# Attention's transposes, mLSTM products and P·V sums share one rotation of four PSUM banks

## The chip, the core and the metric

The kernel runs on one NeuronCore of a Trainium2 chip. Its engines work in parallel, each through its own queue in order: TensorE (PE) with its weight loads (PEld), VectorE (DVE), ScalarE (ACT), GpSimd (POOL), and SyncE (SP), which here issues all DMA transfers. PE writes its results to PSUM, of which this program uses eight banks of 2 KB per partition; DVE and ACT read them out. The metric is the device time of one execution in microseconds (us), lower is better, given as a median over runs.

## The reference, cut to what matters

One layer: a normed and modulated input projection, then two groups of heads side by side (window attention and a two-directional mLSTM), a joint output projection, and a SwiGLU block. The change lies in the part between the two projections:

```python
def window_attention(q, k, v, kc, vc, sink):
    # 8 query heads on 2 key heads, 8 blocks of 128 queries; keys: three neighbouring blocks and 256 context keys
    s_loc = where(valid, einsum(q_block, k_band) * scale, -inf);  s_ctx = einsum(q_block, k_context) * scale
    m = max(s_loc.max, s_ctx.max, sink)
    p_loc, p_ctx = exp(s_loc - m), exp(s_ctx - m)
    inv = 1 / (p_loc.sum + p_ctx.sum + exp(sink - m))
    o = einsum(p_loc * inv, v_band) + einsum(p_ctx * inv, v_context)

def mlstm_chunkwise(q, k, v, ig, lf, state):      # 4 heads, once forward and once backward
    s = einsum(q, k) * w_intra
    num = einsum(s, v) + w_inter * einsum(C, q);  den = s.sum + w_inter * einsum(n, q)
    h = num / max(abs(den), exp(-m))
```

All inputs are float32, 1024 latent tokens and 256 context tokens, width 1024.

## The kernel before, in words

The program has three stretches. The first (to about 293 us of the span) computes modulation, projections, gates and the mLSTM states. The second (about 293 to 457 us) is the attention with the mLSTM outputs, and the first part of the output projection. The third (457 us to the end) is the rest of the output projection and the SwiGLU block, as a Strassen-like product.

In the second stretch the work is cut into 16 **items** (n, g): block of 128 queries n, key head g. For each item `Soft` makes the scores of four heads (L973, L974 on PE into a two-bank tile `s`; the DVE reduction L975 reads it, adds the mask and takes the extreme), the exponentials (ACT, L984) and the division by the row sum (POOL, L989). Two items later `Values.tr` transposes the four heads of one key tile on PE into a bank `pt` (L1002, five tiles `T0` to `T4` per inner item), and copies it to SBUF as `ts_`, even tiles on ACT (L1007), odd ones on DVE (L1005). After both items of a block, `pv` sums the products of P and V for all key tiles into one bank (L1020), and `pv_out` copies that to `mix` on ACT (L1026).

Into the first eight items the mLSTM of blocks 0 to 7 is woven: `ml_scores` (L862, tile `s`, then DVE L867), `ml_values` once per direction (L876 and L880 into two banks `pt`, read by DVE L885 to L887 and by ACT L892 or DVE L894), `ml_norm` (ACT L901 to L903, POOL L904), and `ml_out`, which transposes four heads into one bank `pt` (L910) for DVE L911.

What is issued for one item stands as letters in the plans `PLAN_ML`, `PLAN` and `PLAN13` (T transposes, A scores, N exponentials and division, V mLSTM values, z mLSTM output, M0 and M1 the two calls of `pv` with key tiles 0 to 2 and 3 to 4, O the copy out). From these a scheduler that models the engines sets the order of instructions on each engine, and where it gives a tile one of its buffers. Within one `pv` call the products keep their order. From `msplit(0, 1)` after the loop the order is the program's own.

PSUM before: tag `s` has two buffers of two banks; tag `pt` three of one bank, for transposes and mLSTM products; tag `po` one bank, for the P·V sum. The third stretch uses the same tags, `bank()` for `pt` and `two_banks()` for `pt` with `po`.

Of the kernel before, what the change touches and what calls it, by code (L numbers as in the profile page):

```python
# [9 lines left out]
F32 = mybir.dt.float32  # L10
# [3 lines left out]
PSUM = bass.MemoryType.PSUM  # L14
ADD, SUB, MUL, MAX, MIN = ALU.add, ALU.subtract, ALU.mult, ALU.max, ALU.min

P = 128
D = 1024
# [26 lines left out]
def body(tc, x, ctx, vecs, bcv, bada, gqm, gqf, wada, ws1, ws2, wt, wout, wfi, wfo,  # L45
# [5 lines left out]
    def open_pool(name, bufs=1, side="left", space=None):  # L51
        kw = dict(name=name, bufs=bufs, reuse_waits="tile")
        if space is not None:
            kw["space"] = space
        else:
            kw["side"] = side
        p = tc.tile_pool(**kw)
        return p, p.__enter__()

    def close(p):  # L60
        p[0].__exit__(None, None, None)
# [65 lines left out]
    def R(k, name, shape, dt=F32):  # L127
        t = rp[1].tile([P, 1152 if k < 4 else 1024], dt, name=name, tag=f"r{k}")
        n = int(np.prod(shape))
        v = t[:, 0:n]  # L130
        if len(shape) == 2:
            v = v.rearrange("p (a b) -> p a b", b=shape[1])
        elif len(shape) == 3:
            v = v.rearrange("p (a b c) -> p a b c", b=shape[1], c=shape[2])
        elif len(shape) == 4:
            v = v.rearrange("p (a b c d) -> p a b c d", b=shape[1], c=shape[2], d=shape[3])
        return v
# [160 lines left out]
    for sec in (1, 0):  # L298
# [52 lines left out]
        for q in range(2):  # L351
            t = (hcol, scol)[sec][:, q]
# [70 lines left out]
    for i in range(NI):  # L423
# [16 lines left out]
        if i in (1, 2):  # L440
            b = i - 1
# [138 lines left out]
    def T(i, name):  # L580
        return q2.tile([P, S], F32, name=name, tag=f"s{i}")
# [159 lines left out]
    for j, name in enumerate(TILES):  # L741
# [10 lines left out]
        elif name == "ak":  # L752
# [5 lines left out]
            for a, b, w, dst in ((kr, ks, S, slice(0, S)), (kc[:, 0:L], kc[:, L:2 * L], L, slice(S, S + L))):  # L758
                t = th[64:P] if w == S else kc[64:P, 2 * L:3 * L]
# [7 lines left out]
        elif name.startswith("aq"):  # L767
            t = T(0, f"aq{i}")
# [6 lines left out]
        else:  # L775
            t = R(14 if i == 3 else 15, "so", (S,))
# [39 lines left out]
    pb = psB[1]  # L816
# [4 lines left out]
    qa = atp[1]  # L821
    qa.tile([P, 4, P], F32, name="ts_", tag="pts", bufs=NTS)
    qa.tile([P, 80], F32, name="padq")
    for x_, n in (("pt", 3), ("po", 1)):
        pb.tile([P, 4, P], F32, name=x_, tag=x_, bufs=n)

    def bank():
        return pb.tile([P, 4, P], F32, name="pt", tag="pt", bufs=3)

    def two_banks():  # L830
        return [t.rearrange("p a b -> p (a b)") for t in (bank(), pb.tile([P, 4, P], F32, name="po", tag="po", bufs=1))]


    wts, qps, hss, qz = {}, {}, {}, {}
# [34 lines left out]
    def ml_values(n, d):  # L869
        wt_, qp_, hs = wts[n], qps[n], hss[n][0]  # L870
        s_, r0 = rows_of(n, d)
        cs = state(d, s_)
        pv = [bank().rearrange("p a b -> p (a b)")[:, 0:258].rearrange("p (j v) -> p j v", j=2) for hb in range(2)]
        for j in range(2):
            for hb in range(2):
                pe.matmul(pv[hb][:, j, :], qp_[:, d, j, hb, :], cs[:, j, :], start=j == 0, stop=False,  # L876
                          skip_group_check=j > 0)
        for hb in range(2):
            for j in range(2):
                pe.matmul(pv[hb][:, j, :], wt_[:, d, 2 * j + hb, :], V[:, n, 2 * j + hb, :], start=False, stop=True,  # L880
                          skip_group_check=j > 0)
        dn = qa.tile([P, 2, 2], F32, name="dn", tag="dn", bufs=4)
        for hb in range(2):
            den = pv[hb][:, :, 128]
            dve.tensor_tensor(dn[:, hb], den, emcol[:, r0 + hb:r0 + 4:2], MAX)  # L885
            dve.scalar_tensor_tensor(dn[:, hb], den, -1.0, dn[:, hb], MUL, MAX)
        dve.reciprocal(dn, dn)  # L887
        for hb in range(2):
            for j in range(2):
                t = hs[:, 2 * j + hb]  # L890
                if d == 0:
                    act.activation(t, pv[hb][:, j, 0:128], AF.Copy, scale=dn[:, hb, j:j + 1])  # L892
                else:
                    dve.scalar_tensor_tensor(t, pv[hb][:, j, 0:128], dn[:, hb, j:j + 1], t, MUL, ADD)  # L894
# [11 lines left out]
    def ml_out(n):  # L906
        hs, so = hss.pop(n)
        pt = bank()
        for h in range(4):
            pe.transpose(pt[:, h, :], hs[:, h, :], ident)  # L910
        dve.tensor_tensor(mix[n][:, 4:8, :], pt, so, MUL)  # L911
# [97 lines left out]
    pos = {}  # L1009

    def pv(a, b, ts, more, pin=True):

        ts = [t for t in ts if t < a.nt][::-1]
        first = a.n not in pos
        if first:
            pos[a.n] = pb.tile([P, 4, P], F32, name="po", tag="po", bufs=1)
        for t in ts:
            vt = a.kb0 + t if t < a.nb else NT + t - a.nb
            for g, x_ in ((1, b), (0, a)):
                r = pe.matmul(pos[a.n][64 * g:64 * g + 64], av[:, vt, g], x_.p.pop(t), start=first and t == ts[0],  # L1020
                              stop=not more and t == ts[-1])
                if pin and (t != ts[0] or not g):
                    tc.keep_in_program_order(r)

    def pv_out(n):
        act.copy(mix[n][:, 0:4, :], pos.pop(n))  # L1026
# [3 lines left out]
    for i in range(2):  # L1030
        a = Soft(i)
# [25 lines left out]
    b = None  # L1057
    for i in range(NIT):
        a = Soft(i + 2) if i + 2 < NIT else None
        b0, b = b, Values(i)  # L1060
# [5 lines left out]
        for k in (PLAN_ML[i % 2] if i < NT else PLAN13 if i == NIT - 3 else PLAN[i % 2]).split():  # L1066
            op, n = k[0], int(k[1:] or 0)
            if op == "w" and i + 1 < NT:
                ml_load(i + 1)
            elif op == "T" and n < b.nt:  # L1070
                b.tr(n)
            elif op == "M" and i % 2:
                pv(b0, b, ((0, 1, 2), (3, 4))[n], not n)
            elif op == "O" and i % 2:
                pv_out(b.n)
            elif op == "A" and a:
                a.scores(n)
            elif op == "N" and a:
                a.norm(n)
            elif op == "V" and i < NT:  # L1080
                ml_values(i, n)
            elif op == "x" and i < NT:
                ml_norm(i)
            elif op == "s" and i + 1 < NT:
                ml_scores(i + 1)
            elif op == "z" and 1 <= i <= NT:
                ml_out(i - 1)
            elif op == "l":
                for j in WLOADS.get(i, ()):
                    wout_load(j)  # L1090
            elif op == "p" and i in WSPLIT:
                wout_split(i)
            elif op == "m":
                msplit(0, 0)
                ops_[0] = pb.tile([P, 1024], F32, name="op", tag="s", bufs=2)
            elif op == "P":
                omm(0, 0, range(n, n + 1))
# [17 lines left out]
    msplit(1, 1)  # L1115
    act.preload_act_table_set("sqrt_and_others")
    pv(b, b2, range(4), False, False)
    omm(0, 1, range(3, 4))
    ops_[1] = pb.tile([P, 1024], F32, name="op", tag="s", bufs=2)
    omm(1, 1, range(4))  # L1120
    pv_out(b.n)
    order.__exit__(None, None, None)
    close(atp)
    close(aqp)
    close(akp)
# [142 lines left out]
    def mm_fi(ps, w, b, first):  # L1268

        for k in range(4):  # L1270
            mm3(ps, (w[:, 0, k], w[:, 1, k]), b[k], first and k == 0, k == 3, more=not first)

    def bop(x):
        return [(bh[x][0][:, k], bh[x][1][:, k]) for k in range(4)]

    xv, zb, tm_ = {}, {}, {}

    def fi1(p):
        if p == 2:
            xv[p] = two_banks()  # L1280
        else:
            t = pb.tile([P, D], F32, name=f"xv{p}", tag="s", bufs=2)
            xv[p] = [t[:, 0:512], t[:, 512:D] if p else pb.tile([P, 512], F32, name="xv0b", tag="po", bufs=1)]
        mm_fi(xv[p][0], wops[p]["11"], bop("11"), True)

    def fi2(p):
# [81 lines left out]
    tsums(2, (0, 1))  # L1368
    tsp("T2", 0, 2, "h")
    fi1(0)  # L1370
    opost1(N1)
    es0 = prp[1].tile([P, 512], F32, name="es0", tag="mh", bufs=2)
# [7 lines left out]
    fi2(0)  # L1380
    xstore(N1)
    fi1(1)
    otr(N1)
    close(pC)
# [134 lines left out]
    def gacc(k):  # L1519

        if k < KT:
            dve.scalar_tensor_tensor(gt["acc"], gt[k], csil[:, k, 0:1], gt["acc"], MUL, ADD)
            return
        gps = two_banks()
        for i in range(2):
            sl = slice(i * 512, (i + 1) * 512)
            ps = gps[i]
            for p_ in range(2):
                pe.matmul(ps, gt["one"], gt["hl"][:, p_, sl], start=not p_, stop=p_ == 1)
            gt["p", i] = ps  # L1530
# [193 lines left out]
    for p in range(4, HT):  # L1724
# [39 lines left out]
        if not end:  # L1764
            fm(p + 1, 1)
        else:
            X4 += two_banks()
            t = pb.tile([P, D], F32, name="fx2", tag="s", bufs=2)
            X4 += [t[:, 0:512], t[:, 512:D]]
            fstep(0)  # L1770
# [95 lines left out]
    for s_ in range(1, 8):  # L1866
        q0 = (s_ - 1) * NJ
        KL = 4 if s_ == 7 else 2
        if s_ == 2:
            t = pb.tile([P, D], F32, name="fy0", tag="s", bufs=2)  # L1870
# [35 lines left out]
    close(h2p)  # L1906
    close(prp)
    close(rp)
    close(psB)
    close(cp)  # L1910

# [79 lines left out]
```

## Time and profile before

| | |
|---|---|
| time, median of 3 runs | 1181.61 us (1180.16 to 1184.69) |
| the profiled execution | 1181.65 us, its span 1179.9 us |
| PE busy over the span | 1161.8 us (98%) |
| first stretch, 0 to 293 us | PE busy 286.01 us |
| second stretch, 293 to 457 us | PE busy 159.00 of 164.00 us, DVE 111.27, ACT 115.51, POOL 81.82 |
| third stretch, 457 to 1180 us | PE busy 716.77 of 723.00 us |

A row of a timeline gives start, length, engine, line, operation, output and inputs, and the count of merged instructions; in brackets stands the idle time before it and who ended it. Matmuls overlap, so the time that one takes from the next is read from start to start, not from its length. A float32 P·V product shows as two matmul records of 128x512.

### The profile page before, as it was taken

How to read it: one execution, taken by the hardware profiler on the slowest of the kernel's cores; microseconds unless marked ns; L12 is line 12 of the kernel's file. 1: busy time of each engine (PE TensorE's matmuls, PEld its weight loads, DVE VectorE, ACT ScalarE, POOL GpSimd, SP SyncE). 2: the span in 40 equal slices, each digit the busy share in tenths (PEclk: the TensorE clock that was granted, in tenths of full speed). 3: DMA queues.
4: the chain of work that ended last, by engine and by line, in shares of the span. 5: the costliest groups of instructions: out<-in, count | busy, mean ns of one | idle time of the engine just before them, and what ended most of it. 6: DMA issues, size and time to landing. Idle time of an engine off the chain costs nothing.

```text
span 1179.9 us, 16215 instructions
## 1 busy us (share of the span) xinstructions
PE 1161.8 (98%) x5881; PEld 947.8 (80%) x5881; DVE 781.5 (66%) x1367; ACT 557.7 (47%) x1035; POOL 153.9 (13%) x204
## 2 busy tenths in 40 slices
PE   8899999999999999999999999999999999999997
PEld 3799888778787777888788888888888888888886
DVE  5863768872877752559777767777777755644566
ACT  6743442221776864887443333333333435434543
POOL 1550001225555650000000000000000000000000
PEclk9999999999999999999999999999999999999999
DMA  9611954647887613220233565655654558666853
GB/s 366 218 54 52 391 191 140 216 122 226 217 259 194 200 56 142 90 90 36 98 134 130 202 238 207 221 197 205 221 172 135 178 192 276 201 214 190 303 185 125
DMA packets 101992, 214.89 MB, mean 182 GB/s; under 512 B 10004, under 2 KB 39316, under 8 KB 100504
## 3 DMA queue, kind: packets, MB, share of 16 engines
q1 hardware_dynamic: 101912, 213.85, 54.5%
q8 instruction: 46, 0.75, 0.3%
q14 instruction: 34, 0.28, 0.1%
HBM read 157.19 MB, written 55.97 MB: 181 GB/s over the span
## 4 chain that ended last, share of the span: by engine, by line
PE 89%; DVE 4%; DMA 4%; ACT 1%; issue 1%; SPq 0%; POOL 0%; DVEq 0%; ACTq 0%
PE xv L79 8%; PE xv L78 8%; PE xv L77 8%; PE pt L79 6%; PE pt L77 6%; PE pt L78 6%; PE po L1020 3%; PE t L597 3%; PE t L596 3%; PE t L599 3%; PE pt L1002 3%; PE op L77 3%; PE op L79 2%; PE op L78 2%; PE fx L77 2%; PE slab L77 2%
## 5 line engine op out<-in xcount | busy, mean ns | idle before, releaser
L66 DVE TENSOR_TENSOR fo<-fr,fo 128x1024 fp32r<-128x1024 f32 x77 | 92.9, 1223 | 70.2 <-ACT fo L65 68.4
L65 ACT CAST fo<-fr 128x1024 fp32r<-128x1024 f32 x77 | 79.7, 1053 | 73.9 <-PE pt L79 36.4
L596 PE MATMUL t<-hh,th 128*128 128x512 f32 x208 | 82.4, 396 | 0.0
L597 PE MATMUL t<-hl,th 128*128 128x512 f32 x208 | 82.1, 395 | 0.0
L1397 ACT CAST wS<-wr 128x512 fp32r<-128x512 f32 x88 | 54.3, 624 | 55.2 <-PE pt L79 36.7
L1399 DVE TENSOR_TENSOR wS<-wr,wS 128x512 fp32r<-128x512 f32 x88 | 60.4, 689 | 19.8 <-ACT wS L1397 19.8
L79 PE MATMUL xv<-tT,wS 128*128 128x512 f32 x168 | 65.6, 391 | 0.0
L77 PE MATMUL xv<-tT,wS 128*128 128x512 f32 x168 | 65.6, 390 | 0.0
L78 PE MATMUL xv<-tT,wS 128*128 128x512 f32 x168 | 65.5, 390 | 0.0
L599 PE MATMUL t<-hh,tl 128*128 128x512 f32 x208 | 65.0, 393 | 0.0
L77 PE MATMUL op<-woh,mh 128*128 128x512 f32 x128 | 51.1, 400 | 0.0
L79 PE MATMUL op<-woh,ml 128*128 128x512 f32 x128 | 50.0, 391 | 0.0
L78 PE MATMUL op<-wol,mh 128*128 128x512 f32 x128 | 49.9, 390 | 0.0
L1145 DVE TENSOR_TENSOR wr<-wr 128x512 f32<-128x512 f32 x66 | 45.5, 689 | 1.4
L596 PEld LDWEIGHTS t<-hh,th 128*128 128x128 f32 x208 | 39.1, 188 | 8.3 <-issue 0.3
L597 PEld LDWEIGHTS t<-hl,th 128*128 128x128 f32 x208 | 39.1, 188 | 8.1 <-issue 1.4
L1431 ACT ACTIVATE es<-es 128x512 f32<-128x512 f32 x22 | 14.0, 634 | 66.5 <-DVE es L1148 66.5
L78 PE MATMUL pt<-fo 128*128 128x512 f32 x110 | 42.8, 389 | 0.0
L77 PE MATMUL pt<-fo 128*128 128x512 f32 x110 | 42.8, 389 | 0.0
L79 PE MATMUL pt<-fo 128*128 128x512 f32 x110 | 42.8, 389 | 0.0
L599 PEld LDWEIGHTS t<-hh,tl 128*128 128x128 f32 x208 | 37.3, 188 | 6.6 <-issue 0.5
L973 PE MATMUL s<-k,qh 128*128 128x256 f32 (+1 forms) x128 | 41.7, 337 | 0.6 <-DVE sm L975 0.5
(786 smaller groups left out, 3340.2 us busy)
## 6 DMA issues: line engine op xcount, KB each, us to landing
wr<-in_wfi SPq DMA_DIRECT2D x44, 512.0 KB, 4.7
wb<-in_wada SPq DMA_DIRECT2D x24, 512.0 KB, 5.6
s_d<-a SPq DMA_DIRECT2D x22, 512.0 KB, 7.0
bt<-in_wfo SPq DMA_DIRECT2D x44, 256.0 KB, 3.6
tb_d<-bt SPq DMA_DIRECT2D x11, 1024.0 KB, 3.9
fr<-s_d SPq DMA_DIRECT2D x44, 256.0 KB, 4.2
fr<-tb_d SPq DMA_DIRECT2D x44, 256.0 KB, 4.0
fr<-a_d SPq DMA_DIRECT2D x33, 256.0 KB, 4.3
```

The costliest lines, as they stand in the source:

```text
L65: act.copy(hi, raw)
L66: dve.tensor_tensor(lo, raw, hi.bitcast(F32), SUB)
L77: pe.matmul(ps, a[0], b[0], start=first, stop=False, **kw)
L78: pe.matmul(ps, a[0], b[1], start=False, stop=False, **kw)
L79: pe.matmul(ps, a[1], b[0], start=False, stop=last, **kw)
L596: pe.matmul(o, wh[:, kt], m[0], start=f, stop=False)
L597: pe.matmul(o, wh[:, kt], m[1], start=False, stop=False)
L599: pe.matmul(o, wl[:, kt], m[0], start=False, stop=l)
L973: pe.matmul(o, qh[:, h, :], k2[g][:, kc], start=True, stop=False)
L1145: dve.tensor_tensor(out, a, b, SUB)
L1397: act.copy(w[:, 0], raw)
L1399: dve.tensor_tensor(w[:, 1], raw, w[:, 0].bitcast(F32), SUB)
```

## The change

`po` goes out of the first pool, and a new pool `psT` with four buffers of tag `pt` stands beside it during attention. The P·V sum of a block is now one more tile of that rotation: `pv` takes it with `bank()` when the first batch is issued, it is kept over the second batch, and it is free again once `pv_out` has copied it. The score tiles `s` keep their two buffers, in a pool of their own. When the hand-ordered end of attention is through, `psT` is closed, and a pool `psT2` with three buffers `pt` and one `po` takes its place for the third stretch, whose code is the same but for the name of the tile. No instruction is added or removed on a compute engine; the scheduler, with other buffers to give, puts the second stretch in another order.

```diff
-    for x_, n in (("pt", 3), ("po", 1)):
-        pb.tile([P, 4, P], F32, name=x_, tag=x_, bufs=n)
+    pb.tile([P, 1024], F32, name="s", tag="s", bufs=2)
+    psT = open_pool("psT", space=PSUM)
+    nbk = [4]
+    psT[1].tile([P, 4, P], F32, name="pt", tag="pt", bufs=4)

     def bank():
-        return pb.tile([P, 4, P], F32, name="pt", tag="pt", bufs=3)
+        return psT[1].tile([P, 4, P], F32, name="pt", tag="pt", bufs=nbk[0])
+
+    def po_bank():
+        return psT[1].tile([P, 4, P], F32, name="po", tag="po", bufs=1)

     def two_banks():
-        return [t.rearrange("p a b -> p (a b)") for t in (bank(), pb.tile([P, 4, P], F32, name="po", tag="po", bufs=1))]
+        return [t.rearrange("p a b -> p (a b)") for t in (bank(), po_bank())]
...
         if first:
-            pos[a.n] = pb.tile([P, 4, P], F32, name="po", tag="po", bufs=1)
+            pos[a.n] = bank()
...
     pv_out(b.n)
     order.__exit__(None, None, None)
+    close(psT)
+    psT = open_pool("psT2", space=PSUM)
+    nbk[0] = 3
+    for x_, n in (("pt", 3), ("po", 1)):
+        psT[1].tile([P, 4, P], F32, name=x_, tag=x_, bufs=n)
```

What this does to the order shows at two places on PE. In the changed kernel the lines of this stretch stand five lower in the file: PE's L867 is the former L862, L881 L876, L885 L880, L915 L910, L978 and L979 L973 and L974, L1007 L1002, L1025 L1020. Texts below name lines by their old numbers.

First, PE around `ml_out` of block 3 (`hs3`). Numbers behind a name tell buffers of one name apart. Before:

```order
L1002 MATMUL pt_3530<-vec_59,pr__3138 128x128 x4
L876 MATMUL pt_3537<-cs2_2357,qz0_2731 128x129 x2
L880 MATMUL pt_3537<-V_88,wl4_3429 128x129 x2
L973 MATMUL s_3653<-k2_1_1331,qh_3475 128x384
L974 MATMUL s_3653<-k2_1_1331,ql_3476 128x384
L973 MATMUL s_3653<-k2_1_1331,qh_3475 128x256
L974 MATMUL s_3653<-k2_1_1331,ql_3476 128x256
L876 MATMUL pt_3538<-cs2_2357,qz0_2731 128x129 x2
L880 MATMUL pt_3538<-V_88,wl4_3429 128x129 x2
L1002 MATMUL pt_3562<-vec_59,pr__3138 128x128 x4
L910 MATMUL pt_3569<-vec_59,hs3_3267 128x128 x4
```

And in the changed kernel:

```order
L881 MATMUL pt_3540<-cs2_2357,qz0_2734 128x129 x2
L885 MATMUL pt_3540<-V_88,wl4_3432 128x129 x2
L867 MATMUL s_3606<-mq0_1340,mk0_1338 128x128 x2
L867 MATMUL s_3606<-mq1_1341,mk1_1339 128x128 x2
L978 MATMUL s_3650<-k2_1_1331,qh_3478 128x384
L979 MATMUL s_3650<-k2_1_1331,ql_3479 128x384
L978 MATMUL s_3650<-k2_1_1331,qh_3478 128x256
L979 MATMUL s_3650<-k2_1_1331,ql_3479 128x256
L881 MATMUL pt_3541<-cs2_2357,qz0_2734 128x129 x2
L885 MATMUL pt_3541<-V_88,wl4_3432 128x129 x2
L1007 MATMUL pt_3565<-vec_59,pr__3141 128x128 x4
L915 MATMUL pt_3572<-vec_59,hs3_3270 128x128 x4
```

In both, the mLSTM values of block 4 (two tiles), a transposed key tile and the output of block 3 follow each other: four tiles `pt`, which before have three buffers and now four. The mLSTM scores (L862, now L867) have moved ahead of the group's scores.

Second, PE at the first P·V sum (block 0). Before:

```order
L880 MATMUL pt_3033<-V_88,wl1_2937 128x129 x2
L1020 MATMUL po_3064<-ts__3030,av_91 64x512
L1020 MATMUL po_3064<-ts__2883,av_91 64x512
L973 MATMUL s_3006<-k2_1_1331,qh_2834 128x384
L974 MATMUL s_3006<-k2_1_1331,ql_2835 128x384
L973 MATMUL s_3006<-k2_1_1331,qh_2834 128x256
L974 MATMUL s_3006<-k2_1_1331,ql_2835 128x256
L1002 MATMUL pt_3057<-vec_59,pr__2794 128x128 x4
L1020 MATMUL po_3064<-ts__3023,av_91 64x512
L1020 MATMUL po_3064<-ts__2876,av_91 64x512
L1020 MATMUL po_3064<-ts__2992,av_91 64x512
L1020 MATMUL po_3064<-ts__2845,av_91 64x512
```

And in the changed kernel:

```order
L1007 MATMUL pt_3060<-vec_59,pr__2797 128x128 x4
L885 MATMUL pt_3035<-V_88,wl1_2940 128x129 x2
L1025 MATMUL pt_3067<-ts__3033,av_91 64x512
L1025 MATMUL pt_3067<-ts__2886,av_91 64x512
L1025 MATMUL pt_3067<-ts__3026,av_91 64x512
L1025 MATMUL pt_3067<-ts__2879,av_91 64x512
L1025 MATMUL pt_3067<-ts__2995,av_91 64x512
L1025 MATMUL pt_3067<-ts__2848,av_91 64x512
L885 MATMUL pt_3036<-V_88,wl1_2940 128x129 x2
```

The first batch of this sum stood in two pieces, with scores and a transpose between them, and now stands in one. Over the stretch PE's order has 18 groups of P·V rows before and 15 now, with the same number of products.

More of the change, by code (lines that the diff above doesn't have):

```diff
@@ L1282, in fi1 @@
             t = pb.tile([P, D], F32, name=f"xv{p}", tag="s", bufs=2)
-            xv[p] = [t[:, 0:512], t[:, 512:D] if p else pb.tile([P, 512], F32, name="xv0b", tag="po", bufs=1)]
+            xv[p] = [t[:, 0:512], t[:, 512:D] if p else po_bank().rearrange("p a b -> p (a b)")]
         mm_fi(xv[p][0], wops[p]["11"], bop("11"), True)
@@ L1908, in body @@
     close(rp)
+    close(psT)
     close(psB)
```

## The prediction

> **What bounds the kernel now.** I read the page's busy shares first, then its chain of waits.
>
> ```profile
> PE 1161.8 (98%) x5881; PEld 947.8 (80%) x5881; DVE 781.5 (66%) x1367; ACT 557.7 (47%) x1035; POOL 153.9 (13%) x204
> PE 89%; DVE 4%; DMA 4%; ACT 1%; issue 1%; SPq 0%; POOL 0%; DVEq 0%; ACTq 0%
> ```
>
> PE is busy for 98% of the span and holds 89% of the chain that ended last. An edit that removes no PE work can win only what PE loses in the stretch that it touches. The windows of the three stretches, and the slice of the second in which DVE is fullest (columns: length, then busy time of PE, PEld, DVE, ACT, POOL, granted clock, DMA share, GB/s):
>
> ```profile
> 0.00:293.00 293.00, 286.01 (x1591) 232.76 (x1592) 193.03 (x357) 116.74 (x200) 71.14 (x100) 0.99 0.59 198
> 293.00:457.00 164.00, 159.00 (x1110) 123.82 (x1108) 111.27 (x347) 115.51 (x306) 81.82 (x104) 1.00 0.63 181
> 457.00:1180.00 723.00, 716.77 (x3186) 591.26 (x3182) 477.23 (x663) 325.46 (x529) 0.96 (x1) 1.00 0.51 176
> 320.00:340.00 20.00, 19.38 (x155) 17.43 (x152) 18.15 (x63) 15.93 (x48) 9.80 (x11) 1.00 0.81 226
> ```
>
> In the 164 us of attention PE idles 5.0 us (164.00 - 159.00). The list of PE's waits in that stretch names nearly all of it (waiter, awaited, total us, times, longest):
>
> ```profile
> PE po L1020 <- DVE ts__4746 L1005: 0.8, 1, 0.8
> PE pt L910 <- ACT ts__3567 L1007: 0.8, 1, 0.8
> PE pt L910 <- ACT ts__3893 L1007: 0.8, 1, 0.8
> PE pt L910 <- ACT ts__3233 L1007: 0.5, 1, 0.5
> PE s L973 <- DVE sm L975: 0.5, 1, 0.5
> PE s L974 <- DMA ql<-aq_dl: 0.5, 1, 0.5
> PE pt L910 <- DVE ts__4174 L1005: 0.4, 1, 0.4
> PE pt L1002 <- POOL pr__2742 L989: 0.3, 1, 0.3
> PE s L862 <- DVE sm L975: 0.3, 1, 0.3
> ```
>
> The sum is 4.9 us. Four of the nine have one form: L910, the transposes of `ml_out`, waits for a copy out of another tile `pt`. Their inputs do not come from that copy, so these are waits for a bank. The others wait for data, for the score tiles, or for a DMA. The timeline shows the form:
>
> ```profile
> 356.17 0.60 PE L1002 MATMUL pt<-vec,pr__3138 128*128 128x128 f32 x4
> 356.80 0.59 ACT L1007 COPY ts__3567<-pt 128x512 f32<-128x512 f32 x1 [1.72 <-PE pt L1002]
> 357.53 0.63 PE L910 MATMUL pt<-vec,hs 128*128 128x128 f32 x4 [0.77 <-ACT ts__3567 L1007]
> 382.69 0.63 PE L910 MATMUL pt<-vec,hs 128*128 128x128 f32 x4 [0.77 <-ACT ts__3893 L1007]
> 331.63 0.63 PE L910 MATMUL pt<-vec,hs 128*128 128x128 f32 x4 [0.52 <-ACT ts__3233 L1007]
> 403.72 0.63 PE L910 MATMUL pt<-vec,hs 128*128 128x128 f32 x4 [0.44 <-DVE ts__4174 L1005]
> ```
>
> At 356.17 a key tile is transposed; the next PE instruction must take the very bank just written, because both other banks hold mLSTM values that DVE and ACT are still reading. It stands until the 0.59 us copy is through. The bank of `po` is idle at that moment.
>
> **The change, part by part.** (a) **The fourth bank.** The four waits are 0.77 + 0.77 + 0.52 + 0.44 = 2.50 us. With four buffers the output tile has one of its own while the transposed tile is copied. What is late next is its data: POOL's scaling in `ml_norm`.
>
> ```profile
> 328.52 1.04 POOL L904 TENSOR_TENSOR hs<-hs,sq 128x512 f32<-128x512 f32 x1 [4.84 <-ACT sq L903]
> 402.03 1.04 POOL L904 TENSOR_TENSOR hs<-hs,sq 128x512 f32<-128x512 f32 x1 [2.95 <-ACT sq L903]
> 354.61 0.42 PE L973 MATMUL s<-k,qh 128*128 128x384 f32 x1
> 355.27 0.61 PE L876 MATMUL pt<-cs,qz 128*128 128x129 f32 x4
> ```
>
> For block 7 POOL is done at 403.07, and PE without the bank wait would come at 403.72 - 0.44 = 403.28: free by 0.2 us, and the new order keeps its place. For block 1 POOL is done at 329.56 and PE would come at 331.11, a margin of 1.55 us. But here the new order has two heads' scores and one P·V tile less between the mLSTM values of block 1 and its output. One head's scores take 0.66 us (354.61 to 355.27) and the P·V tile 1.01 (next part), so PE comes 2.33 us earlier and waits 0.78 us for POOL. Gain: 2.50 - 0.78 = 1.72 us.
>
> (b) **P·V in fewer groups.** PE's order has 18 such groups before and 15 now. What a group costs beside its products:
>
> ```profile
> 313.12 0.61 PE L876 MATMUL pt<-cs,qz 128*128 128x129 f32 x4
> 313.57 0.61 PE L880 MATMUL pt<-V,wl 128*128 128x129 f32 x4
> 314.11 0.64 PE L1020 MATMUL po<-ts__3030,av 128*64 128x512 f32 x1
> 315.12 0.44 PE L973 MATMUL s<-k,qh 128*128 128x384 f32 x1
> 316.34 0.64 PE L1020 MATMUL po<-ts__3023,av 128*64 128x512 f32 x1
> 318.20 0.45 PE L973 MATMUL s<-k,qh 128*128 128x384 f32 x1
> ```
>
> A group of one key tile takes 1.01 us (314.11 to 315.12), one of two 1.86 (316.34 to 318.20). A tile is therefore 0.85 and a group 0.16. The way in costs more: four products ahead of it take 0.45 us before other products (313.12 to 313.57) and 0.54 before P·V (313.57 to 314.11), 0.09 more. So 0.25 us a group, and three groups fewer give 0.75 us. This cost is PE's own; nothing hides it.
>
> (c) **The late query load.** Before, the scores of item 3 wait for `ql`:
>
> ```profile
> 310.27 0.41 PE L974 MATMUL s<-k,ql 128*128 128x384 f32 x1 [0.45 <-DMA ql<-aq_dl]
> 310.75 1.03 PE L1002 MATMUL pt<-vec,pr__2794 128*128 128x128 f32 x8
> 311.62 0.61 PE L876 MATMUL pt<-cs,qz 128*128 128x129 f32 x4
> ```
>
> SP's list is the same up to that load. PE's new order does two more key tiles ahead of those scores, 0.87 us by the last two rows, more than the 0.45. The wait goes: 0.45 us.
>
> (d) **What the new order may cost.** It also pulls transposes and mLSTM values forward and pushes scores back. SP's order changes after that load too, but the queries are loaded two items ahead of their scores. The trace cannot show these waits. From below they are nothing. From above I take the 2.50 us that three banks cost. The other waits in the list are nearest, 0.3 to 0.5 each; I take two small ones, 0.6 us.
>
> (e) **The rest.** Holding the sum's bank over both batches takes one of four and leaves three, as before; so the supply is never smaller. Closing `psT` comes after the last copy of attention, and the first transposes of the third stretch wait only for tiles copied several steps earlier: nothing. If that cover failed, one copy, 0.59 us, would show once. No instruction of the third stretch moves.
>
> Sum, from the profiled execution: 1181.65 - 1.72 - 0.75 - 0.45 + 0.60 = **1179.3 us**. That execution is 0.04 us from the median of the runs shown, so I leave it so.
>
> **Rivals.** *The place is taken* (about 1181.2 us). POOL's and ACT's chain behind `ml_out`, not the bank, comes due at most of the four places, and the scheduler, which places tiles by its own estimate, hands out a bank that is still being read. For it: the 0.2 and 1.55 us of margin above. Against it: for block 3 there is time, since its copy wait alone is 0.77 and POOL is not the releaser named. Then (a) falls to 0.25, and (d) rises to 1.0: 1181.65 - 0.25 - 0.75 - 0.45 + 1.0 = 1181.2.
>
> *All of it* (1176.0 us). The new order also hides the waits at the head and the end: 1181.65 - 4.9 - 0.75. Against it: the first two L975 waits and the POOL wait are the pipeline filling, and the 0.8 us at the end is in the hand-written order, which stays.
>
> *Transposes overtake the softmax* (slower, 1185.7 us). Moving scores back shortens the way from a head's last score to its transposes. The chain in between, for item 1, and the same end at item 14:
>
> ```profile
> 302.27 0.73 DVE L975 CUSTOM_DVE_ANT_0 pr__2794<-s,mask,bcr 128x512 f32<-128x512 f32 x1
> 304.65 1.37 POOL L989 TENSOR_SCALAR pr__2794<-pr__2794,sm 128x512 f32<-128x512 f32 x2 [0.70 <-DVE sm L986]
> 308.20 0.60 PE L1002 MATMUL pt<-vec,pr__2794 128*128 128x128 f32 x4
> 433.64 1.36 POOL L989 TENSOR_SCALAR pr__4477<-pr__4477,sm 128x512 f32<-128x512 f32 x2 [2.99 <-DVE sm L986]
> 437.08 0.44 PE L1002 MATMUL pt<-vec,pr__4477 128*128 128x128 f32 x2
> ```
>
> DVE's reading to POOL's end is 3.75 us (302.27 to 306.02), and PE comes 2.18 us after that; at item 14 it is 2.08 us (435.00 to 437.08). It decides once PE's work in between falls under about 3.75 us. A shortage of 1.0 us at each of seven blocks would cost 7.0, in place of the 0.6: 1181.65 - 2.92 + 7.0 = 1185.7. For it: DVE, which heads that chain, is busy 18.15 of 20 us at 320 to 340. Against it: at item 1 the transposes move ahead of one head's scores only, 0.66 of the 2.18 us.
>
> *The clock* (1180.9 us by rows). If the grant fell with more bank switching to the 0.99 of the first window, 159 us of PE work would take 1.6 us longer than forecast. The rows are against it: 1.00 in the window of attention, while three banks already cycle. [...]
>
> **Numbers.** Forecast 0.54, the place taken 0.28, all of it 0.07, overtaking 0.10, the clock 0.01. About half a per cent, 5.9 us, is what a measurement of this kernel can tell from no change: 1175.7 to 1187.5. The forecast and the first rival lie inside, and their own ranges, 1177.5 to 1181 and 1180 to 1183, do too. Faster by more gets 0.04, from the second rival; slower by more 0.05, from half of the third and the clock; the same 0.91. The range goes from the second rival's end, 1176.0, to the first's with the upper bound of (d): 1181.2 + 1.5 + about 1 for the runs' scatter, 1183.8.
>
> **What would show it.** PE's waits in attention: the four L910 rows for ts copies gone, one for POOL's L904 near block 1 at about 0.8 us; no `ql` wait; PE idle 3 us in place of 5.0. P·V in 15 groups, each 0.25 us plus 0.85 a tile. The third stretch 723 us long as before. I am wrong if L1002 shows waits for POOL's L989 beyond item 0, if new waits for copies come to over 2 us, or if the third stretch changes its length.

## The result and the profile after

| | before | after |
|---|---|---|
| time, median of 5 runs each | 1181.80 us (1180.16 to 1184.69) | 1177.44 us (1176.99 to 1177.89) |
| ratio | | 0.9962, 95% interval 0.9947 to 0.9977 |
| profiled execution, its span | 1181.65, 1179.9 us | 1177.44, 1175.7 us |

The forecast was 1179.3 us in a range of 1176.0 to 1183.8. A second measurement beside more runs of the kernel before gave 1177.34 against 1180.72 us, ratio 0.9972 (0.9960 to 0.9983). So the gain is 3.4 to 4.4 us, where 2.3 were forecast.

The window of the second stretch and PE's waits in it, both of the changed kernel:

```profile
293.00:457.00 164.00, 160.81 (x1124) 126.93 (x1123) 110.36 (x349) 118.24 (x311) 80.52 (x102) 1.00 0.63 180
PE s L978 <- DVE sm L980: 1.0, 3, 0.5
PE s L978 <- ACT so L778: 0.9, 1, 0.9
PE pt L1025 <- DVE ts__4749 L1010: 0.9, 1, 0.9
PE s L867 <- DVE sm L980: 0.3, 1, 0.3
```

No row is left in which PE waits for a copy in order to get a bank (L1025 reads `ts__4749` itself). The four rows of `ml_out` (L910, now L915), the row for `ql` and the one for POOL are gone. New is the second row: the first scores wait for ACT's L778. Attention ends earlier now, so the window reaches into the third stretch. A better measure of attention is its length on PE, from the first score to the first output-projection product behind the last P·V sum. The two ends, before:

```profile
293.53 1.09 ACT L778 ACTIVATE so<-t 128x512 f32<-128x512 f32 x2 [6.29 <-PE t L599]
293.56 0.28 PE L973 MATMUL s<-k,qh 128*128 128x256 f32 x1
457.40 0.50 PE L77 MATMUL op<-woh,mh 128*128 128x512 f32 x1
```

And after, with the last row of the first stretch ahead:

```profile
292.62 0.61 PE L599 MATMUL t<-hh,tl 128*128 128x512 f32 x2
293.05 1.08 ACT L778 ACTIVATE so<-t 128x512 f32<-128x512 f32 x2 [6.62 <-PE t L599]
294.19 0.38 PE L978 MATMUL s<-k,qh 128*128 128x256 f32 x1 [0.95 <-ACT so L778]
453.25 0.50 PE L77 MATMUL op<-woh,mh 128*128 128x512 f32 x1
```

Attention takes 163.84 us before (457.40 - 293.56) and 159.06 after: 4.78 less. Behind it both kernels need the same, 1179.9 - 457.40 = 722.5 and 1175.7 - 453.25 = 722.45. Ahead of it the changed kernel loses 1.1 us: from the start of that last L599 row to the first score it takes 1.57 us, and 0.45 before (293.11 to 293.56). The first stretch itself was 0.5 us shorter in this pair of profiles. It was not changed; over the profiles below its end varies by 2.1 us. Together -0.5 + 1.1 - 4.8 = -4.2, the difference of the spans.

### The profile page after: what moved, and what is told of

It reads as the page before. It is cut to its first block, busy times and chain, and to the rows that moved or that the text cites. A ratio compares the mean times of both kernels' runs of the same rounds, so it can differ in the third digit from the quotient of the medians.

```text
span 1175.7 us, 16210 instructions
## 1 busy us (share of the span) xinstructions
PE 1159.6 (99%) x5881; PEld 947.3 (81%) x5881; DVE 778.4 (66%) x1367; ACT 557.2 (47%) x1035; POOL 153.1 (13%) x204
## 4 chain that ended last, share of the span: by engine, by line
PE 90%; DVE 5%; DMA 3%; ACT 1%; issue 1%; SPq 0%; DVEq 0%; POOL 0%
PE xv L79 8%; PE xv L77 8%; PE xv L78 8%; PE pt L79 6%; PE pt L77 6%; PE pt L78 6%; PE pt L1025 3%; PE t L597 3%; PE t L596 3%; PE pt L1007 3%; PE t L599 3%; PE op L77 2%; PE op L78 2%; PE op L79 2%; PE fx L77 2%; PE slab L77 2%
## 5 line engine op out<-in xcount | busy, mean ns | idle before, releaser
L599 PE MATMUL t<-hh,tl 128*128 128x512 f32 x208 | 65.0, 393 | 0.0
L978 PE MATMUL s<-k,qh 128*128 128x256 f32 (+1 forms) x128 | 42.4, 340 | 2.0 <-DVE sm L980 1.0
L599 PEld LDWEIGHTS t<-hh,tl 128*128 128x128 f32 x208 | 37.3, 188 | 6.6 <-issue 0.5
```

Source lines behind the costliest of these rows:

```text
L599: pe.matmul(o, wl[:, kt], m[0], start=False, stop=l)
L978: pe.matmul(o, qh[:, h, :], k2[g][:, kc], start=True, stop=False)
```

## The experiments

Line numbers in each profile are those of that kernel, a few lines off from the others. The kernels were measured in three groups, each beside the kernel before, which took 1180.73, 1180.72 and 1180.69 us there. The measured numbers:

| kernel | time, us | ratio to before | length of attention, us |
|---|---|---|---|
| before, again | 1180.73 | | 163.15 |
| after, again | 1177.34 | 0.9972 (0.9960 to 0.9983) | 159.05 |
| sharing undone | 1181.60 | 1.0006 (0.9996 to 1.0015) | 163.04 |
| `ml_out` in `po` | 1181.42 | 1.0003 (0.9994 to 1.0012) | 163.68 |
| P·V held together | 1180.59 | 1.0002 (0.9993 to 1.0010) | 163.20 |
| three shared banks | 1189.06 | 1.0068 (1.0055 to 1.0081) | 170.08 |
| pools exchanged | 1176.59 | 0.9966 (0.9952 to 0.9980) | 159.12 |
| last sum in four groups | 1182.05 | 1.0012 (1.0003 to 1.0020) | see there |
| pools exchanged, tile 0 first | 1175.83 | 0.9959 (0.9946 to 0.9971) | 158.15 |
| longer POOL scaling | 1178.34 | 0.9982 (0.9973 to 0.9992) | 159.24 |

### Both kernels once more

> The changed kernel once more, to see how far the length of attention and of the first stretch vary from one profile to the next. If they are the program's own: attention 159.06 us within 0.1, the four L915 rows without a wait, and the 0.95 us before the first score again; the first stretch's last product, at 292.85 us against 293.33 before, may vary by half a us, since no instruction of it was moved.

> The kernel before once more, to see how far its length of attention (163.84 us) and the start of attention (first score at 293.56 us) vary between profiles. If the stretch is the program's own: 163.84 within 0.2, the same four L910 rows; the start may vary by a us, as it did between the other runs (292.2 to 294.4).

The changed kernel repeats to 0.01 us, the wait of 0.9 us at the start with it. The kernel before does not: 163.15 for 163.84. Its waits on PE, from 285 to 470 us:

```profile
PE po L1020 <- DVE ts__4746 L1005: 0.8, 1, 0.8
PE pt L910 <- ACT ts__3567 L1007: 0.8, 1, 0.8
PE pt L910 <- ACT ts__3893 L1007: 0.8, 1, 0.8
PE pt L910 <- ACT ts__3233 L1007: 0.5, 1, 0.5
PE s L973 <- DVE sm L975: 0.5, 1, 0.5
PE pt L910 <- DVE ts__4174 L1005: 0.4, 1, 0.4
PE pt L1002 <- POOL pr__2742 L989: 0.3, 1, 0.3
PE s L862 <- DVE sm L975: 0.3, 1, 0.3
```

The four L910 rows are the program's own. The wait for `ql`, counted in the prediction as 0.45 us of gain, is not there: the DMA was late in one execution and not in the other. Set beside this profile, attention gains 163.15 - 159.06 = 4.1 us, and with the 1.1 lost ahead of it 3.0.

### The sharing undone

> The changed kernel with the sharing undone: scores in a pool of their own as in the change, but psT holds three banks pt and one po, and the P·V sum is in po. PE's order is that of the kernel before. Measured by the time and by the length of attention on PE, from its first score to the first output-projection product behind the last P·V sum: 163.84 us before (293.56 to 457.40), 159.06 after (294.19 to 453.25). Theory (the gain is the fourth bank in the rotation): the L910 waits are back, 2.5 us of idle, length about 163.8, time that of the kernel before within 1 us; and since the scores lie in the banks that the first stretch used last, PE again waits about 0.95 us for ACT's L778 before the first score. Rival (the gain comes from the scores' banks apart, or from where the tiles lie in PSUM): length about 159, time near 1177.4.

```diff
-    nbk = [4]
-    psT[1].tile([P, 4, P], F32, name="pt", tag="pt", bufs=4)
+    nbk = [3]
+    for x_, n in (("pt", 3), ("po", 1)):
+        psT[1].tile([P, 4, P], F32, name=x_, tag=x_, bufs=n)
...
-            pos[a.n] = bank()
+            pos[a.n] = po_bank()
```

The waits on PE of this kernel:

```profile
PE s L979 <- ACT so L778: 0.9, 1, 0.9
...
PE pt L916 <- ACT ts__3897 L1013: 0.8, 1, 0.8
PE pt L916 <- ACT ts__3571 L1013: 0.8, 1, 0.8
PE pt L916 <- ACT ts__3237 L1013: 0.5, 1, 0.5
...
PE pt L916 <- DVE ts__4178 L1011: 0.4, 1, 0.4
```

The theory held: the length is that of the kernel before (163.04, 163.15), the same four waits are back, and the time is not better. Since the order is the old one too, this run shows what banks and order do together. Scores in banks apart do nothing for attention. They bring the L778 row, which stands in every kernel that has the scores in banks 0 to 3. In each of these the first transposes no longer wait 0.3 us for POOL; so that row went with the late start of the scores, not with the new order.

### One more bank at `ml_out` alone

> The kernel before with one edit: the mLSTM output of blocks 1, 3, 5 and 7 is transposed into po, which is idle at that place, in place of a bank of the rotation. Theory (the four L910 waits were bank waits and each costs its idle time plus about 0.16 us of refilling PE): they go, length of attention 163.84 - 3.1 = 160.7 us or a little less, time about 1178.6. By the prediction's own term for these waits (1.72 of 2.50, a POOL wait in the place of one): length 162.1, time 1180. Rival (what follows the bank is POOL's chain, so the wait only changes its name): length over 163, time within 0.7 of the kernel before.

```diff
-        pt = bank()
+        pt = pb.tile([P, 4, P], F32, name="po", tag="po", bufs=1) if n % 2 else bank()
```

Around block 3, the timeline of this kernel, and below it two rows of its waits:

```profile
354.94 0.60 PE L910 MATMUL po<-vec,hs 128*128 128x128 f32 x4
356.88 0.60 PE L1002 MATMUL pt<-vec,pr__3138 128*128 128x128 f32 x4
357.51 0.58 ACT L1007 COPY ts__3567<-pt 128x512 f32<-128x512 f32 x1 [2.18 <-PE pt L1002]
358.15 0.71 PE L876 MATMUL pt<-cs,qz 128*128 128x129 f32 x4 [0.68 <-ACT ts__3567 L1007]
...
PE pt L876 <- ACT ts__3567 L1007: 0.7, 1, 0.7
PE pt L876 <- ACT ts__3893 L1007: 0.7, 1, 0.7
```

The theory fell. All four L910 waits went, and the time stayed (1.0003). The rival's numbers came true, but not its reason: no wait for POOL's scaling appears. At two of the four places the wait only changed hands: the output finds `po` free and goes early, and the next taker of a bank, the mLSTM values L876 of block 4, stands in front of the same copy of `ts__3567`. At these two it is the rotation of three that is too short, not one transposition that stands badly. Two waits of 0.7 do not make up the whole 2.5 us: in this profile the first transposes waited 0.3 us longer for POOL and `ql` was late again by 0.3, and about a us more lies in pieces of under 0.25 us in the new order, which I have not traced.

### P·V held together

> The kernel before with the first product of each P·V sum held to the others, so that PE's order has 16 P·V groups in place of 18, with po and three banks as before. Theory (a group costs 0.2 to 0.25 us of PE): length of attention shorter by 0.4 to 0.5 us by the groups, 163.4, with the four L910 waits still there; time about 1181.2. Rival (the part of the gain that is no bank wait, about 2 us, comes from the groups, 0.7 us each): length 162.4, time 1180.2.

```diff
-                if pin and (t != ts[0] or not g):
+                if pin and (first or t != ts[0] or not g):
```

Inconclusive. Three of the four L910 waits stand as they were; at block 1 PE waits 0.40 us at the same place, and the profile names no releaser. But the length (163.20) is that of the repeated kernel before, 163.15, where 0.4 to 0.5 less was expected. One of the 16 groups is a sum whose two products per tile were put apart, with mLSTM values between them; these two start within 0.01 us of each other in the kernel before, 1.01 us from start to start together (322.07 to 323.08), and apart took 1.01 (317.89 to 318.90) and 1.00 (320.88 to 321.88). So the saving of two groups was used up by that: from start to start all P·V rows take 35.9 us here and 35.4 in the repeated kernel before. The run decides nothing on the price of a group.

### Three shared banks

> The changed kernel with three banks in the shared rotation in place of four, one bank of PSUM left unused. PE's order then has 14 P·V groups. Theory (the supply of banks sets the waits): with the sum holding one of three, two are left, waits for copies come back at most tiles under it: length of attention over 164 us, time 1182 or more. Rival (the order, with its fewer groups, gives the gain, and three would do): length 159 to 160, time 1177 to 1178.

```diff
-    nbk = [4]
-    psT[1].tile([P, 4, P], F32, name="pt", tag="pt", bufs=4)
+    nbk = [3]
+    psT[1].tile([P, 4, P], F32, name="pt", tag="pt", bufs=3)
```

Four of the rows in which PE waits in attention:

```profile
PE pt L1025 <- DVE ts__4048 L1010: 0.8, 1, 0.8
PE pt L1025 <- DVE ts__3718 L1010: 0.8, 1, 0.8
PE pt L915 <- ACT ts__3236 L1012: 0.8, 1, 0.8
PE pt L915 <- ACT ts__3570 L1012: 0.8, 1, 0.8
```

The theory held by far: 11.0 us longer than with four, though this order has the fewest P·V groups (14). The L1025 rows shown take other tiles as input than those whose copies they wait for, so they too wait for a bank. Ten such waits come to 5.6 us, where the kernel before has four and 2.5; scores wait 1.7 us longer for DVE than with four, and the rest of the 11.0 is not divided. Fewer groups without the bank are no gain; sharing pays only with the fourth.

### The pools' places exchanged

> The changed kernel with the places of the two pools in PSUM exchanged: the shared rotation in banks 0 to 3, the scores in banks 4 to 7, as in the kernel before. Order and number of buffers are those of the change. In the changed kernel the first score waits 0.95 us for ACT's L778, which reads banks 0 and 1, the last ones of the first stretch. Theory (that wait is a loss on the path): it goes, the time from the first stretch's last product (L599) to the first score falls from 1.34 us to about 0.23 as before, and the time by 0.9 us to 1176.5. Rival (the wait hides behind the softmax chain, which starts no earlier): the wait turns up behind the first scores, at L978 or at the first transposes, and the time stays at 1177.4 within 0.4.

```diff
-        else:
-            kw["side"] = side
+        kw["side"] = side
...
-    psB = open_pool("psB", space=PSUM)
+    psB = open_pool("psB", side="right", space=PSUM)
```

The last row of the first stretch (two products) and the first score of this kernel:

```profile
292.06 0.62 PE L598 MATMUL t<-hh,tl 128*128 128x512 f32 x2
292.52 0.28 PE L977 MATMUL s<-k,qh 128*128 128x256 f32 x1
```

There is no wait in it: the two rows start 0.46 us apart, as before the change (0.45). The time falls by 0.75 us, from 1177.34 to 1176.59, measured beside each other; 0.9 was expected, and the runs of the two overlap a little (1176.93 to 1177.64 against 1175.77 to 1177.17). The rows are clearer. The rival is right that a wait turns up behind: the first transposes wait 0.3 us for POOL again. But from the start of that last row to the first transposes it is 5.40 us here (292.06 to 297.46) and 6.42 in the changed kernel (292.62 to 299.04), so 1.0 us is won all the same. Attention keeps its 159.1. So the change has a cost that no part of the prediction had: with the scores' pool opened first, the scores lie where the first stretch writes its last sums.

### The last sum in four groups

> The changed kernel with the last P·V sum, whose place is written by hand, in four groups in place of one, six output-projection products between them; nothing else moves. It measures what a group costs. Prediction's term: 0.25 us for each of three more groups, 0.75 us in all, time 1178.2. Rival (0.7 us a group, so that three groups fewer would make up the whole part of the gain that is no wait): 2.1 us, time 1179.5. Other rival (a group costs nothing): 1177.4.

```diff
-    pv(b, b2, range(4), False, False)
+    pv(b, b2, (3,), True, False)
     omm(0, 1, range(3, 4))
     ops_[1] = pb.tile([P, 1024], F32, name="op", tag="s", bufs=2)
-    omm(1, 1, range(4))
+    for k in range(3):
+        pv(b, b2, (2 - k,), k < 2, False)
+        omm(1, 1, range(k, k + 1))
+    omm(1, 1, range(3, 4))
```

From the first P·V product to the 24th output product, in the changed kernel:

```profile
449.66 0.61 PE L1025 MATMUL pt<-ts__4749,av 128*64 128x512 f32 x1 [0.88 <-DVE ts__4749 L1010]
458.60 0.39 PE L79 MATMUL op<-woh,ml 128*128 128x512 f32 x1
```

And in this one, then ACT's two rows and PE's behind it, and last three windows of 2 us (the seventh number is the granted clock):

```profile
449.79 0.61 PE L1025 MATMUL pt<-ts__4749,av 128*64 128x512 f32 x1 [0.88 <-DVE ts__4749 L1010]
459.87 0.39 PE L79 MATMUL op<-woh,ml 128*128 128x512 f32 x1
...
458.72 0.59 ACT L1031 COPY mix<-pt 128x512 f32<-128x512 f32 x1 [9.18 <-PE pt L1025]
459.20 1.03 ACT L1210 ACTIVATE t<-op 128x1024 f32<-128x1024 f32 x1
464.19 0.50 PE L79 MATMUL op<-woh,ml 128*128 128x512 f32 x1 [2.12 <-DVE ml L66]
...
462.00:464.00 2.00, 0.07 (x1) 0.00 (x0) 1.91 (x3) 0.43 (x1) 0.00 (x0) 1.00 0.00 0
464.00:466.00 2.00, 1.81 (x5) 1.45 (x6) 0.30 (x2) 1.74 (x4) 0.00 (x0) 0.70 0.82 266
466.00:468.00 2.00, 2.00 (x6) 1.59 (x5) 0.69 (x1) 0.93 (x2) 0.00 (x0) 0.50 1.00 354
```

The same products take 8.94 us in one group and 10.08 in four: 1.14 us for three groups, 0.38 each among output products, where the prediction had 0.25 among scores and transposes. The time rose by 4.7 us, though, because the sum's end is late. ACT kept the order of its queue: L1210, the first step after the output projection of block 0, came behind the copy of the sum at 458.72 and started at 459.20, though its input was done at 452.5, and by the time DVE has its `ml` ready PE has been idle for 2.12 us. So the run's time says nothing on a group; its rows do.

### The wait at the end

> The changed kernel with the pools' places in PSUM exchanged, as in the run before of that kind (1176.59 us), and one more edit: the last P·V sum, whose order is written by hand, begins with key tile 0 in place of tile 3. Before and after the change PE waits there 0.8 to 0.9 us for DVE's copy of tile 3, which was transposed just ahead; no other instruction moves. Theory (a wait that any other work of PE can fill): three tiles take about 2.6 us, the wait goes, attention is 0.9 to 1.0 us shorter than 159.12, time 1175.6. Rival (the copies of the other tiles, or the products behind the sum, come due at the same moment): the wait moves to L77 or to a second copy, time 1176.6.

```diff
-    pv(b, b2, range(4), False, False)
+    pv(b, b2, (3, 2, 1, 0), False, False)
```

PE's waits in this kernel, from 285 to 470 us:

```profile
PE s L977 <- DVE sm L979: 1.0, 3, 0.5
PE s L866 <- DVE sm L979: 0.3, 1, 0.3
PE pt L1006 <- POOL pr__2745 L993: 0.3, 1, 0.3
```

The wait is gone, attention is 0.97 us shorter (158.15), and the time 1175.83 us, 0.76 less than with the pools exchanged alone, which was measured in another group. This is the fastest version found: 0.9959 of the kernel before (0.9946 to 0.9971).

### A longer scaling on POOL

> The changed kernel with POOL's scaling in ml_norm made longer: a multiplication by one, about 1.04 us, ahead of it, so that each mLSTM output is ready later; the result is the same. It asks whether POOL's chain is what would be late next behind the four outputs, as the prediction had it. In the changed kernel POOL's scaling ends 2.94, 0.56, 0.99, 0.81, 1.71, 2.58, 2.17 and 0.06 us ahead of PE's L915 for blocks 0 to 7. Theory (the prediction's step, with these margins): at unchanged order four of the eight come to wait, 0.48 + 0.05 + 0.23 + 0.98 = 1.7 us of idle and 0.16 us more each, time about 1179.7; the scheduler knows of the longer operation and may give part of that back by moving L915. Rival (POOL's chain has slack, PE finds other work): no wait for POOL's scaling in attention's list, time 1177.4 within 0.5.

```diff
+        pool.tensor_scalar(hs, hs, 1.0, 1.0, MUL, MUL)
         pool.tensor_tensor(hs, hs, hcast(sq), MUL)
```

PE's waits in this kernel, and POOL's two rows of `ml_norm` for block 5:

```profile
PE s L979 <- ACT so L778: 0.9, 1, 0.9
PE pt L1026 <- DVE ts__4757 L1011: 0.9, 1, 0.9
PE s L979 <- DVE sm L981: 0.8, 2, 0.5
PE s L867 <- DVE sm L981: 0.3, 1, 0.3
...
373.03 0.62 POOL L909 TENSOR_SCALAR hs<-hs 128x512 f32<-128x512 f32 x1 [1.16 <-ACT junk L906]
374.81 1.04 POOL L910 TENSOR_TENSOR hs<-hs,sq 128x512 f32<-128x512 f32 x1 [1.16 <-ACT sq L908]
```

None of the waits is for POOL, and attention is only 0.2 us longer. The rival held for the waits; its bound on the time (0.5 us) was passed with 1.0 (measured in another group), of which attention's length explains 0.2 and the rest is not found. But the edit delayed the outputs less than meant. The added operation took 0.62 us, not 1.04, and ran at several blocks, as in the rows shown, while POOL still had to wait for ACT's `sq`. At three blocks POOL had had 2.8 to 2.9 us of idle time ahead of the scaling. Counted from the first score, POOL's end came 0.2 to 1.5 us later. At blocks 2 and 3 PE's new order puts the output later; at blocks 1 and 7 PE starts it 0.05 us behind POOL's end. So POOL's chain is just in time there, without a wait that the list shows; what a truly later output would cost is not shown.

## Why the prediction was right, and where not

**What bounds it** was right: what was won is idle time and switching on PE inside attention; behind it nothing moved.

**(a) The fourth bank.** Right in its mechanism, the cause is shown from both sides: undone, the four waits return; with three shared banks the waits for a bank are ten. Wrong in size, twice. The term was 1.72 us, 2.50 of idle less a wait of 0.78 for POOL's L904 at block 1. That wait did not come:

```profile
326.41 1.04 POOL L909 TENSOR_TENSOR hs<-hs,sq 128x512 f32<-128x512 f32 x1
328.01 0.60 PE L915 MATMUL pt<-vec,hs 128*128 128x128 f32 x4
```

POOL ends at 327.45, 0.56 us ahead of PE. The step that failed set PE 2.33 us earlier and left POOL at its old 329.56. But POOL's chain starts from PE's own mLSTM values, which moved forward with the rest: POOL came 2.1 us earlier too. Where it is nearest, at block 7, POOL ends 0.06 us ahead of PE. And each wait cost more than its idle time. Before, four transposes run to the next start in 0.43 us:

```profile
447.92 0.60 PE L1002 MATMUL pt<-vec,pr__4477 128*128 128x128 f32 x4
448.35 0.60 PE L1002 MATMUL pt<-vec,pr__4555 128*128 128x128 f32 x4
```

With the wait at block 3 they take 1.36 (356.17 to 357.53): 0.93 lost, where the list says 0.77. The list counts idle time from the end of the last product. In the two rows above, without a wait, the next one started 0.17 us before that end (448.35, the end at 448.52). Counted from start to start the four waits are 3.1 us, not 2.50.

**(b) Fewer groups.** 0.75 us was about right: from start to start all P·V rows take 35.35 us before and 34.88 after, 0.47 less, and with the prediction's 0.09 on the way into each of three groups it is 0.74. Set beside the kernel with the sharing undone, whose start is the same, attention gains 4.0 us (163.04 to 159.05). The waits' 3.1 and the groups' 0.74, less 0.8 in (d), explain 3.1 of that; about 0.9 is left, which I put down to many small changes of order between kinds of product. That part was not in the sum, and no run divides it.

**(c) The late query load.** Wrong as a gain of the change: the wait came and went between profiles of the same order, 0.45 us in one and none in the other. A DMA wait that stands in one profile is no term of a sum.

**(d) New costs.** 0.60 us was near for what it meant. Scores waiting for DVE cost 0.8 us more, counted from start to start: two more waits, 0.32 and 0.16 us of idle time. The L778 wait of 0.95 us is missing: the prediction looked at how many banks each tile had, not at which. Part (e) asked that question for the end of attention and not for its start.

**The rivals.** "The place is taken" fell: no wait for POOL and none for a bank of the rotation is left. "All of it" fell in its reason, since the waits for DVE at the head and the wait at the end stand. Its 1176.0 us was reached only with two more edits (1175.83). "Overtaking" fell: no L1002 row waits for POOL. The granted clock of attention stayed at 1.00, so "The clock" fell too. No run shows a time lengthened by a lower grant in attention, and 1180.9 us would lie inside the half per cent: the clock's part in the chance of a slower result rests on nothing that the runs show.

So the forecast was 1.9 us too high by the first measurement and about 1 by the second, with terms too small in (a) and the small changes beside (b), and one cost missed. That it came so near is in part luck: (a) was 1.4 us too small and the 0.9 beside (b) was left out, while 0.45 was counted that the change does not give and 1.1 ahead of the first score was overlooked. The effect lies within the half per cent.

## What to carry to other kernels

A wait for a buffer belongs to the rotation, not to the instruction that shows it: giving that one instruction another bank handed the wait to the next taker at two of four places here, and won nothing. When pools are rearranged, ask which banks the work ahead used last, not only how many there are: this cost 0.95 us of idle time here. When PE moves forward, move every chain that starts from PE with it before looking for the next bound (POOL came 2.1 us earlier here), and put a wait down from start to start (0.93 us at block 3, where the list has 0.77).

## What was not expected of the hardware

In the kernel with the last sum in four groups, PE idled for 2.12 us; behind that its granted clock was 0.70 and 0.50 in two windows of 2 us, and about eight products started 0.43 us apart in place of 0.23, some 1.6 us more than the wait itself. This is one profile. Behind the waits of attention, 0.95 us at most, nothing like it shows: 1.00 in every window of 2 us from 285 to 469 us, before and after the change.

The length of the wait alone does not decide it. In the first stretch of the kernel before, the granted clock was 0.86, 0.50 and 0.79 in the three windows from 34 to 40 us, behind a wait of 0.95 us that ended at 34.02, and 1.00 from 44 to 48 us, behind one of 1.46 us that ended at 44.97. In the changed kernel the first of these waits was 0.95 us as well, and the clock 1.00 from 34 to 40 us. What lowers it is not shown.
